# Moving the 32x32 inverses of a gated delta rule, and the transfers behind them, to GpSimd

## The chip, the cores and the metric

The kernel runs on one core of one Trainium2 chip. Times are device microseconds of a whole launch; each is the median of several runs. A core has five engines that work side by side, each with its own instruction order: TensorE (PE, matrix products; PEld is its weight load), VectorE (DVE), ScalarE (ACT), GpSimd (POOL) and SyncE (SP). An engine that issues a DMA does so in its own order, so an issue that waits holds up whatever stands behind it on that engine.

## The reference, cut to what matters

The reference is a two-block transformer on one sequence of 256 tokens, width 1024, all in f32: a gated DeltaNet layer, a convolutional MLP, sliding-window attention, a second MLP, and then a block with further mixers and an FFN. The change sits in the DeltaNet layer at the start. Its core solves one unit lower triangular system per chunk and head:

```python
    m = jnp.where(strict, jnp.einsum('bnhcd,bnhsd->bnhcs', k_beta, k) * decay, 0.0)
    eye = jnp.broadcast_to(jnp.eye(c, dtype=f32), m.shape)
    t_mat = lax.linalg.triangular_solve(m + eye, eye, left_side=True, lower=True,
                                        unit_diagonal=True)
    u = jnp.einsum('bnhcs,bnhse->bnhce', t_mat, v_beta)
    ...
    o = rmsnorm(o, out_norm_w) * jax.nn.silu(z)
    return o.reshape(bsz, t, GDN_V_DIM).astype(hn.dtype) @ w_out
```

The layer has 16 heads of 128. The kernel works with two chunks of 128 tokens.

## The kernel before

**Weights and products.** All weights arrive as 362 chunks of 128x1024 floats, in the order in which PE uses them, issued by SP (L172). ACT rounds each chunk to a high half wh (L186), DVE subtracts to get the low half wl (L187, two operands in SBUF), and every product of an activation with a weight is three matmuls (`mm3`, L249 to L251): xh·wh, xl·wh, xh·wl. The buffers let a few chunks run ahead of PE.

**Side work.** What is no weight product runs in generators. `tick` advances each of them by one `yield`; `w` calls it once per four weight tiles of 128 columns, which is twelve matmuls. So a stage that says `for _ in range(N): yield` lets N such pieces of weight work go ahead of it in the program. A tile scheduler then orders each engine's instructions from the program's order and the data that each needs. Nothing on the chip waits for a tick; the chip waits for data only.

**The inverse.** The q, k, v and z parts of `w_in` follow each other in the order of `ORDER`. From k, `x_stage` computes for each head three 128x128 blocks XA[:, h, 0..2] (chunk 0, the cross block, chunk 1). A 128x128 block is inverted from its four 32x32 diagonal blocks upward. `x_stage` stores the 4·2·16 diagonal blocks to DRAM s1, and `inv_stage` reads them back as NT with one block per partition (128 partitions, 32x32 each). Then 31 steps of substitution follow, each a product (fst, L757) and an addition into TI (L759), with one tick after each. TI is copied transposed to TP (L764). Both go to DRAM (s2, s3; `Q[2]`) and come back into place in 14 loads (`Q[3]`), eight into XA and six into T64, which lies in the tile h. `QS` says which engine issues each: `QS = "sgss"` means SP for s1, the two stores and the 14 loads, and GpSimd for NT.

**After the inverse.** `WINV` ticks later `st["inv"]` is set, and `chain(q4)` runs four times, for four heads each. It joins the blocks to 64 and then 128: y1p (L823) and z1p (L833, L834), with Y1 between them on ACT and DVE, then y2p and z2p. It then forms y0p, x10p, y1p (L879), the outputs o0p and o1p (L890 to L894), the gate and normalization on ACT and DVE, and the transposes otp (L921), whose results feed the product with `w_out`. `a_stage` runs beside it: one kq product (L729, L730) per pair of heads. The gate z goes through DRAM: GpSimd stores zt to wzd (L803) and loads it back as wzog (L886). A pool t2 of six buffers is shared by the convolution (cy), vt, zt, Y1, Y2 and r1.

Of the kernel before, what the change touches and what calls it, by code (L numbers as in the profile page):

```python
# [9 lines left out]
F32 = mybir.dt.float32  # L10
# [3 lines left out]
AF = mybir.ActivationFunctionType  # L14
ALU = mybir.AluOpType
# [4 lines left out]
P = 128  # L20
T = 256
# [98 lines left out]
CZ = 2  # L120
WSSB = 9
WVTP = 6
WINV = 10
ACCN = 4
SY1 = 5
SY2 = 5
# [8 lines left out]
XK = 0  # L135
NY = 4
NP = 2
QS = "sgss"
PINS = {1: 0, 3: 1}
ORDER = "qqzqqzvvvvvvzvvz"  # L140

# [1 line left out]
class Builder:  # L143
# [432 lines left out]
    def gdn_body(self, gp, x):  # L576
        nc, tc, sp = self.nc, self.tc, self.sp
# [3 lines left out]
        blk = lambda b: slice(32 * b, 32 * b + 32)  # L581
        ev2 = lambda b: b.rearrange("p (a t) -> p a t", a=2)
# [13 lines left out]
        ea = gp.tile([P, 1], F32, tag="ea", name="ea")  # L596
        fac = gp.tile([P, 5, 32], F32, tag="fac", name="fac")
        var, rk, irk, negc, rk2 = (fac[:, i] for i in range(5))
        XA = gp.tile([P, 16, 3, P], F32, tag="XA", name="XA")
        EA = gp.tile([P, 16, 3, P], F32, tag="EA", name="EA")  # L600
        vn = gp.tile([P, 2, 2048], F32, tag="vn", name="vn")
        st = {"bg": False, "kss": 0, "qss": 0, "X": 0, "v": 0, "inv": False, "z": 0, "A": 0, "lev": 0, "og": 0, "step": 0}
# [86 lines left out]

        Q = [{"s": nc.sync, "a": nc.scalar, "g": nc.gpsimd}[c] for c in QS]  # L690

        def x_stage():
            while st["kss"] < 4 or not st["bg"]:
                yield
            factors(0)
            for j in range(8):
                kk = self.bank("kk")
                nc.tensor.matmul(kk[:, 0:T], kT[:, j, 0:P], kT[:, j], start=True, stop=True)
                nc.tensor.matmul(kk[:, T:384], kT[:, j, P:], kT[:, j, P:], start=True, stop=True)
                for h in (2 * j, 2 * j + 1):  # L700
                    rp = self.bank("rp")
                    nc.tensor.matmul(rp[:, :384], identr[:, h : h + 1].to_broadcast([P, P]), gch, start=True, stop=False)
                    nc.tensor.matmul(rp[:, :384], identb, mask3b, start=False, stop=True)
                    nc.scalar.activation(EA[:, h, 0], rp[:, 0:128], AF.Exp, bias=bg[:, 0, 32 + h : 33 + h])
                    nc.scalar.activation(EA[:, h, 1], rp[:, 128:256], AF.Exp, bias=bg[:, 0, 64 + h : 65 + h])
                    nc.scalar.activation(EA[:, h, 2], rp[:, 256:384], AF.Exp, bias=bg[:, 1, 32 + h : 33 + h])
                    nc.vector.scalar_tensor_tensor(XA[:, h, 0:2], ev2(kk[:, 0:T]), negc[:, h : h + 1], EA[:, h, 0:2], ALU.mult, ALU.mult)
                    nc.vector.scalar_tensor_tensor(XA[:, h, 2], kk[:, T:384], negc[:, 16 + h : 17 + h], EA[:, h, 2], ALU.mult, ALU.mult)
                st["X"] = j + 1
                if j % 4 == 3:  # L710
                    H = slice(2 * j - 6, 2 * j + 2)
                    for b in range(4):
                        for tt in range(2):
                            Q[0].dma_start(s1[b, tt, H].rearrange("h s t -> s h t"), XA[blk(b), H, 2 * tt, blk(b)])
                if j % 4 != 3:
                    yield
                else:
                    for _ in range(4):
                        yield
# [19 lines left out]
        s1 = self.dp.tile([4, 2, 16, 32, 32], F32, name="s1")  # L739
        s2 = self.dp.tile([4, 2, 16, 32, 32], F32, name="s2")  # L740
        s3 = self.dp.tile([4, 2, 16, 32, 32], F32, name="s3")
        T64 = self.h.rearrange("p a t -> p (a t)").rearrange("p (a h c) -> p a h c", a=2, h=16)

        def inv_stage():
            while st["X"] < 8:
                yield
            NT = t4([P, 32, 32], "NT")
            TI = t4([P, 32, 32], "TI")
            Q[1].dma_start(NT, s1.rearrange("b c h s t -> (b c h) s t"))
            nc.gpsimd.memset(TI, 0.0)  # L750
            nc.gpsimd.memset(TI.rearrange("p a b -> p (a b)")[:, 0:1024:33], 1.0)
            for _ in range(INVW):
                yield
            for j in range(31):
                m = 31 - j
                tmp = gp.tile([P, 256], F32, tag="fst", bufs=1, name="fst")[:, : m * (j + 1)].rearrange("p (a b) -> p a b", a=m)
                nc.vector.tensor_tensor(tmp, NT[:, j, j + 1 :].unsqueeze(2).to_broadcast([P, m, j + 1]),  # L757
                                        TI[:, j, 0 : j + 1].unsqueeze(1).to_broadcast([P, m, j + 1]), ALU.mult)
                nc.vector.tensor_tensor(TI[:, j + 1 :, 0 : j + 1], TI[:, j + 1 :, 0 : j + 1], tmp, ALU.add)  # L759
                st["step"] = j + 1  # L760
                if INVS(j):
                    yield
            TP = t4([P, 32, 32], "TP")
            nc.vector.tensor_copy(TP.rearrange("p c i -> p i c"), TI)  # L764
            Q[2].dma_start(s3.rearrange("b c h s t -> (b c h) s t"), TP)
            Q[2].dma_start(s2.rearrange("b c h s t -> (b c h) s t"), TI)
            nc.gpsimd.memset(T64[0:32, :, :, 32:64], 0.0)
            for b in range(4):
                for tt in range(2):
                    Q[3].dma_start(XA[blk(b), :, 2 * tt, blk(b)], s3[b, tt].rearrange("h c i -> c h i"))  # L770
                    if b < 3:
                        c = (0, 32, 0)[b]
                        Q[3].dma_start(T64[blk(b), tt, :, c : c + 32], s2[b, tt].rearrange("h i c -> i h c"))
            for _ in range(WINV):
                yield
            st["inv"] = True
# [31 lines left out]
        hs = lambda i: slice(i * P, i * P + P)  # L808
        oks = {}

        def chain(q4):
            while not (st["inv"] and st["v"] >= 2 * q4 + 2 and st["lev"] >= q4):
                yield
            H = slice(4 * q4, 4 * q4 + 4)
            heads = range(4 * q4, 4 * q4 + 4)
            cs = slice(512 * q4, 512 * q4 + 512)
            Y1 = t2([P, 2, 4, 32], "Y1")
            b = self.bank("y1p")
            bv = b[:, 0:256].rearrange("p (a h c) -> p a h c", a=2, h=4)
            for tt in range(2):  # L820
                for i, h in enumerate(heads):
                    for j in (0, 2):
                        nc.tensor.matmul(bv[blk(j + 1), tt, i], XA[blk(j), h, 2 * tt, blk(j + 1)], T64[blk(j), tt, h, 0:32], start=True, stop=True)  # L823
            nc.scalar.activation(Y1[blk(1)], bv[blk(1)], AF.Copy)
            nc.vector.tensor_copy(Y1[blk(3)], bv[blk(3)])
            for _ in range(CY):
# [1 line left out]
            b = self.bank("z1p")  # L828
            bv = b.rearrange("p (k a h c) -> p k a h c", k=2, a=2, h=4)
            for tt in range(2):  # L830
                for i, h in enumerate(heads):
                    for j in (0, 2):
                        nc.tensor.matmul(bv[blk(j), 0, tt, i], Y1[blk(j + 1), tt, i], XA[blk(j + 1), h, 2 * tt, blk(j + 1)], start=True, stop=True)  # L833
                    nc.tensor.matmul(bv[blk(1), 1, tt, i], XA[blk(1), h, 2 * tt, blk(1)], Y1[blk(1), tt, i], start=True, stop=True)  # L834
            nc.scalar.activation(T64[blk(1), :, H, 0:32], bv[blk(1), 1], AF.Copy)
            for tt in range(2):
                nc.vector.tensor_copy(XA[blk(0), H, 2 * tt, blk(1)], bv[blk(0), 0, tt])
                nc.scalar.activation(XA[blk(2), H, 2 * tt, blk(3)], bv[blk(2), 0, tt], AF.Copy)
            for _ in range(CY):
                yield  # L840
            lo, hi = slice(0, 64), slice(64, 128)
            Y2 = t2([P, 2, 4, 64], "Y2")
            b = self.bank("y2p")
            bv = b.rearrange("p (a h c) -> p a h c", a=2, h=4)
            for tt in range(2):
                for i, h in enumerate(heads):
                    nc.tensor.matmul(bv[hi, tt, i], XA[lo, h, 2 * tt, hi], T64[lo, tt, h], start=True, stop=True)  # L847
            nc.scalar.activation(Y2[hi], bv[hi], AF.Copy)
            for _ in range(CY):
                yield  # L850
            b = self.bank("z2p")
            bv = b.rearrange("p (a h c) -> p a h c", a=2, h=4)
            for tt in range(2):
                for i, h in enumerate(heads):
                    nc.tensor.matmul(bv[lo, tt, i], Y2[hi, tt, i], XA[hi, h, 2 * tt, hi], start=True, stop=True)  # L855
            for tt in range(2):
                nc.vector.tensor_copy(XA[lo, H, 2 * tt, hi], bv[lo, tt])
            st["lev"] += 1
            for _ in range(CY):
                yield  # L860
# [2 lines left out]
            y = t4([P, 2, 512], "yy")  # L863
# [6 lines left out]
                yield  # L870
            b = self.bank("x10p")
            for i, h in enumerate(heads):
                nc.tensor.matmul(b[:, hs(i)], XA[:, h, 1], y[:, 0, hs(i)], start=True, stop=True)
            nc.vector.tensor_tensor(r1, b, vn[:, 1, cs], ALU.add)
            for _ in range(CZ):
                yield
            b = self.bank("y1p")
            for i, h in enumerate(heads):
                nc.tensor.matmul(b[:, hs(i)], XA[:, h, 2], r1[:, hs(i)], start=True, stop=True)  # L879
            nc.scalar.activation(y[:, 1], b, AF.Copy)  # L880
            while st["A"] < 2 * q4 + 2 or st["z"] < 2 * q4 + 2:
                yield
# [1053 lines left out]
```

## Time and profile before

| what | value |
|---|---|
| median of 3 runs | 1217.02 us (1215.78 to 1218.51) |
| the profiled execution's own time | 1216.23 us |
| its span, first to last instruction | 1214.4 us |
| granted TensorE clock, mean | 0.997 |
| PE busy | 1188.7 us, 98% of the span |
| DVE busy | 895.2 us, 74% |
| ACT busy | 687.7 us, 57% |
| POOL busy | 20.4 us, 2% |

The span lies 1.83 us inside the execution's own time. PE is nearly always busy; its idle time, and what ended each piece of it, is what a change beside it can alter. The averages cover 1214 us, while the inverse occupies some 60 to 80 us near the start, so the stretch from 100 to 210 us has to be read by itself. In the rows below a timeline gives start, duration, engine, line, operation, out<-in, and in brackets the idle time before it with what ended it.

### The profile page before, as it was taken

To read this page: it belongs to the slowest core of one execution; us is meant where nothing else is said; L and a number is where in the kernel's file an instruction comes from. 1 tells how busy PE (TensorE), PEld (TensorE's weight loads), DVE (VectorE), ACT (ScalarE), POOL (GpSimd) and SP (SyncE) were. 2 spreads that over 40 slices of the span, in tenths; PEclk is the share of its full clock that TensorE was granted. 3 is DMA by queue.
4 is the path that set the end of the run, shared out by engine and by line. 5 is a ranking of instruction groups with operands and counts; after the bars stand their busy time and mean duration, and the time that the engine had idled before them with its cause. 6 is when DMAs were issued, how large, how long until landed. Compare 5 with 4: busy or idle time off the path is not lost.

```text
span 1214.4 us, 23416 instructions
## 1 busy us (share of the span) xinstructions
PE 1188.7 (98%) x9368; PEld 1125.4 (93%) x9368; DVE 895.2 (74%) x1680; ACT 687.7 (57%) x1170; POOL 20.4 (2%) x47
## 2 busy tenths in 40 slices
PE   7999989999999999999999999999999999999997
PEld 6989878999999999889999999889789999999996
DVE  6978976668877778878977778756756567655555
ACT  5785547546655556656755556754465445444443
POOL 1000000000000000000000000000000000000000
PEclk9999999999999999999999999999999999999999
DMA  6546365355555557435555564364255563555552
GB/s 222 179 132 216 125 192 183 124 157 168 199 184 182 187 179 243 126 115 161 190 188 183 187 191 158 112 207 134 87 161 173 188 234 118 186 179 187 189 179 83
DMA packets 68318, 206.01 MB, mean 170 GB/s; under 512 B 18198, under 2 KB 18342, under 8 KB 67953
## 3 DMA queue, kind: packets, MB, share of 16 engines
q1 hardware_dynamic: 65600, 194.77, 50.3%
q0 software_dynamic: 2608, 9.75, 2.2%
q8 instruction: 73, 1.20, 0.4%
q14 instruction: 37, 0.29, 0.1%
HBM read 199.75 MB, written 4.74 MB: 168 GB/s over the span
## 4 chain that ended last, share of the span: by engine, by line
PE 92%; DVE 4%; ACT 2%; DMA 1%; issue 1%; SPq 0%; DVEq 0%; ACTq 0%
PE pb L249 21%; PE pb L250 20%; PE pb L251 20%; PE acc L249 7%; PE acc L250 7%; PE acc L251 7%; DVE wl L187 1%; PE pt L1138 1%; PE ssb L669 1%; DMA wr<-wall 0%; DMA h<-xT 0%; PE z2p L855 0%; PE y2p L847 0%; PE kv L1542 0%; PE csum L366 0%
## 5 line engine op out<-in xcount | busy, mean ns | idle before, releaser
L187 DVE TENSOR_TENSOR wl<-wr,wh 128x1024 fp32r<-128x1024 f32 x362 | 441.5, 1223 | 193.7 <-ACT wh L186 192.3
L186 ACT ACTIVATE wh<-wr 128x1024 fp32r<-128x1024 f32 x362 | 381.6, 1057 | 338.3 <-issue 101.1
L251 PE MATMUL pb<-xh,wl 128*128 128x256 f32 x1224 | 345.6, 283 | 3.9 <-DVE wl L187 3.9
L249 PE MATMUL pb<-xh,wh 128*128 128x256 f32 x1224 | 347.8, 284 | 0.6 <-ACT xh L569 0.6
L250 PE MATMUL pb<-xl,wh 128*128 128x256 f32 x1224 | 345.5, 282 | 0.2 <-DVE xl L570 0.2
L249 PEld LDWEIGHTS pb<-xh,wh 128*128 128x128 f32 x1224 | 231.7, 189 | 2.8 <-issue 1.3
L251 PEld LDWEIGHTS pb<-xh,wl 128*128 128x128 f32 x1224 | 229.7, 188 | 4.5 <-DVE wl L187 4.5
L250 PEld LDWEIGHTS pb<-xl,wh 128*128 128x128 f32 x1224 | 230.1, 188 | 0.5 <-DVE xl L570 0.4
L249 PE MATMUL pb<-fh,wh 128*128 128x256 f32 x416 | 118.3, 285 | 0.0
L250 PE MATMUL pb<-fl,wh 128*128 128x256 f32 x416 | 117.5, 283 | 0.1
L251 PE MATMUL pb<-fh,wl 128*128 128x256 f32 x416 | 116.6, 281 | 0.0
L249 PE MATMUL acc<-ah,wh 128*128 128x256 f32 x352 | 98.7, 280 | 0.0
L251 PE MATMUL acc<-ah,wl 128*128 128x256 f32 x352 | 98.5, 280 | 0.0
L250 PE MATMUL acc<-al,wh 128*128 128x256 f32 x352 | 98.5, 280 | 0.0
L249 PEld LDWEIGHTS pb<-fh,wh 128*128 128x128 f32 x416 | 77.9, 188 | 1.4 <-issue 0.4
L250 PEld LDWEIGHTS pb<-fl,wh 128*128 128x128 f32 x416 | 78.1, 188 | 1.1 <-DVE fl L436 0.3
L251 PEld LDWEIGHTS pb<-fh,wl 128*128 128x128 f32 x416 | 78.9, 190 | 0.0
L977 DVE SCALAR_TENSOR_TENSOR fy<-fpad,cols,fy 128x256 f32<-128x256 f32 x176 | 73.6, 478 | 0.0
L249 PE MATMUL pb<-wh,xh 128*128 128x512 f32 (+1 forms) x176 | 70.5, 402 | 0.0
L250 PE MATMUL pb<-wl,xh 128*128 128x512 f32 (+1 forms) x176 | 68.1, 387 | 0.5 <-DVE wl L187 0.5
L251 PE MATMUL pb<-wh,xl 128*128 128x512 f32 (+1 forms) x176 | 68.0, 387 | 0.0
L249 PEld LDWEIGHTS acc<-ah,wh 128*128 128x128 f32 x352 | 66.9, 190 | 0.0
(437 smaller groups left out, 2091.2 us busy)
## 6 DMA issues: line engine op xcount, KB each, us to landing
wr<-wall SPq DMA_DIRECT2D x362, 512.0 KB, 3.6
wzd<-zt POOLq DMA_DIRECT2D x8, 256.0 KB, 3.0
wzog<-wzd POOLq DMA_DIRECT2D x4, 512.0 KB, 5.2
bias<-bd POOLq DMA_DIRECT2D x4, 512.0 KB, 7.7
h<-xT SPq DMA_DIRECT2D x4, 256.0 KB, 4.0
h<-xT POOLq DMA_DIRECT2D x1, 1024.0 KB, 5.9
wrow<-wrow POOLq DMA_DIRECT2D x1, 1024.0 KB, 10.0
out_dram<-mw SPq DMA_DIRECT2D x4, 256.0 KB, 2.0
```

What stands on the lines that cost most here:

```text
L186: nc.scalar.activation(hi, r, AF.Copy)
L187: i = nc.vector.tensor_tensor(lo, r, hi.bitcast(F32), ALU.subtract)
L249: mm(out, ah, bh, start=start, stop=False, skip_group_check=skip)
L250: mm(out, ah, bl, start=False, stop=False, skip_group_check=skip)
L251: mm(out, al, bh, start=False, stop=stop, skip_group_check=skip)
L669: nc.tensor.matmul(ssb[:, c : c + 1], sq[:, i, tt * P : tt * P + P], self.ones[:, 0:1], start=True, stop=True)
L977: nc.vector.scalar_tensor_tensor(y[:, i], u[:, i, j : j + T], w(j), y[:, i], ALU.mult, ALU.add)
L1138: nc.tensor.transpose(pt[:, j * P : j * P + P], S[:, i, j * P : j * P + P], self.ident)
```

## The change

The 62 operations of the substitution and the transposing copy run on GpSimd instead of DVE. `QS` becomes "sggg": the stores to s2 and s3 and the loads behind them are issued by GpSimd instead of SP. XA is stored with the block index ahead of the head and with the two chunks' blocks next to each other, so one load fills both chunks: 7 loads of 128 KB in place of 14 of 64 KB. All index expressions follow (`2 * tt` becomes `tt`, the cross block is 2 instead of 1). `WINV` goes from 10 to 16.

```diff
-WINV = 10
+WINV = 16
-QS = "sgss"
+QS = "sggg"
...
-        XA = gp.tile([P, 16, 3, P], F32, tag="XA", name="XA")
+
+        XAb = gp.tile([P, 3, 16, P], F32, tag="XA", name="XA")
+        XA = XAb.rearrange("p k h c -> p h k c")
...
-                nc.vector.tensor_tensor(tmp, NT[:, j, j + 1 :].unsqueeze(2).to_broadcast([P, m, j + 1]),
+                nc.gpsimd.tensor_tensor(tmp, NT[:, j, j + 1 :].unsqueeze(2).to_broadcast([P, m, j + 1]),
                                         TI[:, j, 0 : j + 1].unsqueeze(1).to_broadcast([P, m, j + 1]), ALU.mult)
-                nc.vector.tensor_tensor(TI[:, j + 1 :, 0 : j + 1], TI[:, j + 1 :, 0 : j + 1], tmp, ALU.add)
+                nc.gpsimd.tensor_tensor(TI[:, j + 1 :, 0 : j + 1], TI[:, j + 1 :, 0 : j + 1], tmp, ALU.add)
...
-            nc.vector.tensor_copy(TP.rearrange("p c i -> p i c"), TI)
+            nc.gpsimd.tensor_copy(TP.rearrange("p c i -> p i c"), TI)
             Q[2].dma_start(s3.rearrange("b c h s t -> (b c h) s t"), TP)
             Q[2].dma_start(s2.rearrange("b c h s t -> (b c h) s t"), TI)
...
-                for tt in range(2):
-                    Q[3].dma_start(XA[blk(b), :, 2 * tt, blk(b)], s3[b, tt].rearrange("h c i -> c h i"))
-                    if b < 3:
-                        c = (0, 32, 0)[b]
-                        Q[3].dma_start(T64[blk(b), tt, :, c : c + 32], s2[b, tt].rearrange("h i c -> i h c"))
+                Q[3].dma_start(XAb[blk(b), 0:2, :, blk(b)].rearrange("p k h c -> p (k h) c"), s3[b].rearrange("a h c i -> c (a h) i"))
+                if b < 3:
+                    c = (0, 32, 0)[b]
+                    Q[3].dma_start(T64[blk(b), :, :, c : c + 32].rearrange("p a h c -> p (a h) c"), s2[b].rearrange("a h i c -> i (a h) c"))
...
-                        nc.tensor.matmul(bv[blk(j + 1), tt, i], XA[blk(j), h, 2 * tt, blk(j + 1)], T64[blk(j), tt, h, 0:32], start=True, stop=True)
+                        nc.tensor.matmul(bv[blk(j + 1), tt, i], XA[blk(j), h, tt, blk(j + 1)], T64[blk(j), tt, h, 0:32], start=True, stop=True)
```

Lines of the changed kernel are one or two higher than before (y1p L824, z1p L834). On SP, before, the two stores and the 14 loads stand among the weight loads (s_208 and s_209 are the DRAM tiles s2 and s3):

```order
L172 DMA wr_1867<-wall 128x1024
L766 DMA s_208<-TI 128x1024
L765 DMA s_209<-TP 128x1024
L172 DMA wr_1892<-wall 128x1024
L773 DMA h<-s_208 32x16x32
L770 DMA XA<-s_209 32x16x32 x2
L773 DMA h<-s_208 32x16x32
L770 DMA XA<-s_209 32x16x32
```

After, only weight loads are left on SP. On GpSimd, after, the substitution begins behind the clearing of TI, around a pair of stores of z:

```order
L752 MEMSET TI 128x1024
L753 MEMSET TI 128x32
L759 ISA
L759 TENSOR_TENSOR fst<-NT,TI 128x31
L804 DMA wzd<-zt 128x512
L761 TENSOR_TENSOR TI<-TI,fst 128x31
L804 DMA wzd<-zt 128x512
L759 TENSOR_TENSOR fst<-NT,TI 128x60
```

The first addition stands behind one of these stores and the second product behind the other. On the same engine, after, this is the end of the substitution:

```order
L761 TENSOR_TENSOR TI<-TI,fst 128x31
L766 COPY TP<-TI 128x32x32
L768 DMA s_208<-TI 128x1024
L767 DMA s_209<-TP 128x1024
L774 DMA h<-s_208 32x32x32
L771 DMA XA<-s_209 32x32x32 x2
L774 DMA h<-s_208 32x32x32
L771 DMA XA<-s_209 32x32x32
L774 DMA h<-s_208 32x32x32
L771 DMA XA<-s_209 32x32x32
L804 DMA wzd<-zt 128x512 x2
L887 DMA wzog<-wzd 128x1024 x2
```

The copy, two stores and seven loads now stand in one queue, and the next stores of z and the loads of the gate stand behind them. On PE, before, 15 of the 16 matmuls of the first join (y1p, of h and XA) follow the sixth of the eight kq at a distance of three weight products (pb), and the first z1p comes at once behind them:

```order
L729 MATMUL kq<-qT,kT 128x256
L730 MATMUL kq<-qT,kT 128x128
L249 MATMUL pb<-xh,wh_1919 128x256
L250 MATMUL pb<-xl,wh_1919 128x256
L251 MATMUL pb<-xh,wl_1920 128x256
L823 MATMUL y1p<-h,XA 32x32 x15
L833 MATMUL z1p<-XA,Y_1976 32x32
```

On PE, after, the same join follows the seventh kq:

```order
L731 MATMUL kq<-qT,kT 128x256
L732 MATMUL kq<-qT,kT 128x128
L824 MATMUL y1p<-h,XA 32x32 x16
L249 MATMUL pb<-xh,wh_1974 128x256
L250 MATMUL pb<-xl,wh_1974 128x256
L251 MATMUL pb<-xh,wl_1975 128x256
L249 MATMUL pb<-wh_2023,xh 128x512
```

The first join moved from the sixth kq to the seventh, at once behind it, and weight products come between it and z1p. Further on, on PE, before, weight products stand between the first output o0p and its companion o1p (o0p and o1p are the two outputs of a group of heads; two more groups of six follow before otp):

```order
L890 MATMUL o0p<-yy,EA 128x128 x4
L855 MATMUL z2p<-XA,Y_2288 64x64 x8
L823 MATMUL y1p<-h,XA 32x32 x16
L249 MATMUL pb<-wh_2202,xh 128x512
L250 MATMUL pb<-wl_2203,xh 128x512
L251 MATMUL pb<-wh_2202,xl 128x512
```

On PE, after, at the same place:

```order
L848 MATMUL y2p<-h,XA 64x64 x8
L880 MATMUL y1p<-r_2281,XA 128x128 x4
L891 MATMUL o0p<-yy,EA 128x128 x4
L856 MATMUL z2p<-XA,Y_2338 64x64 x8
L824 MATMUL y1p<-h,XA 32x32 x16
L894 MATMUL o1p<-yy,EA 128x128
L895 MATMUL o1p<-yy,EA 128x128
```

From o0p to otp there is no weight product any more; the three groups of six stand ahead of it.

## Rows read from the trace of the kernel before

**Rows 1.** Page: part 1 (busy, share, instructions) and chain shares by engine

```profile
PE 1188.7 (98%) x9368; PEld 1125.4 (93%) x9368; DVE 895.2 (74%) x1680; ACT 687.7 (57%) x1170; POOL 20.4 (2%) x47
...
PE 92%; DVE 4%; ACT 2%; DMA 1%; issue 1%; SPq 0%; DVEq 0%; ACTq 0%
```

**Rows 2.** Timeline of PE, 139 to 179 (start, us, what; idle before, releaser)

```profile
139.51 0.39 PE L251 MATMUL pb<-xh,wl 128*128 128x256 f32 x1 [1.47 <-DVE wl L187]
...
154.03 0.51 PE L250 MATMUL pb<-wl,xh 128*128 128x512 f32 x1 [0.49 <-DVE wl L187]
...
160.60 0.33 PE L789 MATMUL vtp<-ident,vt 128*128 128x128 f32 x1 [1.14 <-ACT vt L651]
...
169.75 0.21 PE L833 MATMUL z1p<-XA,Y 32*32 32x32 f32 x1 [0.46 <-ACT Y L824]
...
178.07 0.39 PE L251 MATMUL pb<-xh,wl 128*128 128x256 f32 x1 [1.72 <-DVE wl L187]
```

**Rows 3.** Windows: per stretch length, busy of PE, PEld, DVE, ACT, POOL

```profile
100.00:130.00 30.00, 30.00 (x235) 29.03 (x234) 28.07 (x68) 16.75 (x25) 1.08 (x2) 1.00 0.60 190
130.00:160.00 30.00, 27.50 (x175) 24.08 (x173) 29.72 (x79) 15.14 (x25) 0.00 (x0) 1.00 0.50 153
```

**Rows 4.** Lines of DVE, 100 to 160 (busy, mean ns; idle)

```profile
L187 DVE TENSOR_TENSOR wl<-wr,wh 128x1024 fp32r<-128x1024 f32 x18 | 21.7, 1216 | 1.3 <-ACT wh L186 1.3
...
L759 DVE TENSOR_TENSOR TI<-TI,fst 128x31 f32<-128x31 f32 (+15 forms) x31 | 10.4, 336 | 0.2
...
L757 DVE TENSOR_TENSOR fst<-NT,TI 128x31 f32<-128x31 f32 (+15 forms) x31 | 10.3, 333 | 0.1
...
L764 DVE COPY TP<-TI 128x1024 f32<-128x1024 f32 x1 | 1.1, 1146 | 0.0
```

**Rows 5.** Timeline of SP's DMA queue, 150 to 163

```profile
150.67 0.33 SPq L766 DMA_DIRECT2D s<-TI  x1
...
162.99 86.68 SPq L172 DMA_DIRECT2D wr<-wall  x19
```

**Rows 6.** Timeline of POOL, the instructions nearest to the change

```profile
7.13 0.30 POOL L589 CAST identb<-ident 128x128 bf16<-128x128 f32 x1 [5.54 <-DMA ident<-cst]
...
21.08 0.66 POOL L588 CAST mask3b<-mask 128x384 bf16<-128x384 f32 x1
...
97.17 0.15 POOL L751 MEMSET TI<- 128x32 f32 x1
...
106.27 0.54 POOL L803 DMA_DIRECT2D wzd<-zt  x1 [0.16 <-issue]
```

**Rows 7.** DVE beside the cast; line L187, ns min/median/max

```profile
21.31 1.52 DVE L187 TENSOR_TENSOR wl<-wr,wh 128x1024 fp32r<-128x1024 f32 x1
...
L187 DVE TENSOR_TENSOR wl<-wr,wh x362: 1202/1225/1520, 10.7 to 1198.2; 128x1024 fp32r<-128x1024 f32 x181
```

**Rows 8.** Line L1045: issue of a transfer of 512 runs

```profile
L1045 POOL DMA_DIRECT2D bias<-bd x4: 748/754/800, 469.9 to 472.2; - x4
```

**Rows 9.** DMA view: issues, KB each, median us to landing

```profile
s<-TI SPq DMA_DIRECT2D x1, 512.0 KB, 3.6
...
XA<-s SPq DMA_DIRECT2D x8, 64.0 KB, 3.9
...
h<-s SPq DMA_DIRECT2D x6, 64.0 KB, 2.9
```

**Rows 10.** Timeline of PE: seventh kq, then o0p and otp

```profile
175.29 0.38 PE L729 MATMUL kq<-qT,kT 128*128 128x256 f32 x1
...
195.56 1.06 PE L890 MATMUL o0p<-yy,EA 128*128 128x128 f32 x8
...
198.24 0.50 PE L249 MATMUL pb<-wh,xh 128*128 128x512 f32 x1
...
199.74 0.38 PE L893 MATMUL o1p<-yy,EA 128*128 128x128 f32 x2
...
208.52 0.66 PE L921 MATMUL otp<-ident,wzog 128*128 128x128 f32 x4
```

More of the change, by code (lines that the diff above doesn't have):

```diff
@@ L706, in x_stage @@
                     nc.scalar.activation(EA[:, h, 2], rp[:, 256:384], AF.Exp, bias=bg[:, 1, 32 + h : 33 + h])
-                    nc.vector.scalar_tensor_tensor(XA[:, h, 0:2], ev2(kk[:, 0:T]), negc[:, h : h + 1], EA[:, h, 0:2], ALU.mult, ALU.mult)
-                    nc.vector.scalar_tensor_tensor(XA[:, h, 2], kk[:, T:384], negc[:, 16 + h : 17 + h], EA[:, h, 2], ALU.mult, ALU.mult)
+                    nc.vector.scalar_tensor_tensor(XA[:, h, 0:3:2], ev2(kk[:, 0:T]), negc[:, h : h + 1], EA[:, h, 0:2], ALU.mult, ALU.mult)
+                    nc.vector.scalar_tensor_tensor(XA[:, h, 1], kk[:, T:384], negc[:, 16 + h : 17 + h], EA[:, h, 2], ALU.mult, ALU.mult)
                 st["X"] = j + 1
@@ L713, in x_stage @@
                         for tt in range(2):
-                            Q[0].dma_start(s1[b, tt, H].rearrange("h s t -> s h t"), XA[blk(b), H, 2 * tt, blk(b)])
+                            Q[0].dma_start(s1[b, tt, H].rearrange("h s t -> s h t"), XA[blk(b), H, tt, blk(b)])
                 if j % 4 != 3:
@@ L832, in chain @@
                     for j in (0, 2):
-                        nc.tensor.matmul(bv[blk(j), 0, tt, i], Y1[blk(j + 1), tt, i], XA[blk(j + 1), h, 2 * tt, blk(j + 1)], start=True, stop=True)
-                    nc.tensor.matmul(bv[blk(1), 1, tt, i], XA[blk(1), h, 2 * tt, blk(1)], Y1[blk(1), tt, i], start=True, stop=True)
+                        nc.tensor.matmul(bv[blk(j), 0, tt, i], Y1[blk(j + 1), tt, i], XA[blk(j + 1), h, tt, blk(j + 1)], start=True, stop=True)
+                    nc.tensor.matmul(bv[blk(1), 1, tt, i], XA[blk(1), h, tt, blk(1)], Y1[blk(1), tt, i], start=True, stop=True)
             nc.scalar.activation(T64[blk(1), :, H, 0:32], bv[blk(1), 1], AF.Copy)
             for tt in range(2):
-                nc.vector.tensor_copy(XA[blk(0), H, 2 * tt, blk(1)], bv[blk(0), 0, tt])
-                nc.scalar.activation(XA[blk(2), H, 2 * tt, blk(3)], bv[blk(2), 0, tt], AF.Copy)
+                nc.vector.tensor_copy(XA[blk(0), H, tt, blk(1)], bv[blk(0), 0, tt])
+                nc.scalar.activation(XA[blk(2), H, tt, blk(3)], bv[blk(2), 0, tt], AF.Copy)
             for _ in range(CY):
@@ L846, in chain @@
                 for i, h in enumerate(heads):
-                    nc.tensor.matmul(bv[hi, tt, i], XA[lo, h, 2 * tt, hi], T64[lo, tt, h], start=True, stop=True)
+                    nc.tensor.matmul(bv[hi, tt, i], XA[lo, h, tt, hi], T64[lo, tt, h], start=True, stop=True)
             nc.scalar.activation(Y2[hi], bv[hi], AF.Copy)
@@ L854, in chain @@
                 for i, h in enumerate(heads):
-                    nc.tensor.matmul(bv[lo, tt, i], Y2[hi, tt, i], XA[hi, h, 2 * tt, hi], start=True, stop=True)
+                    nc.tensor.matmul(bv[lo, tt, i], Y2[hi, tt, i], XA[hi, h, tt, hi], start=True, stop=True)
             for tt in range(2):
-                nc.vector.tensor_copy(XA[lo, H, 2 * tt, hi], bv[lo, tt])
+                nc.vector.tensor_copy(XA[lo, H, tt, hi], bv[lo, tt])
             st["lev"] += 1
@@ L872, in chain @@
             for i, h in enumerate(heads):
-                nc.tensor.matmul(b[:, hs(i)], XA[:, h, 1], y[:, 0, hs(i)], start=True, stop=True)
+                nc.tensor.matmul(b[:, hs(i)], XA[:, h, 2], y[:, 0, hs(i)], start=True, stop=True)
             nc.vector.tensor_tensor(r1, b, vn[:, 1, cs], ALU.add)
@@ L878, in chain @@
             for i, h in enumerate(heads):
-                nc.tensor.matmul(b[:, hs(i)], XA[:, h, 2], r1[:, hs(i)], start=True, stop=True)
+                nc.tensor.matmul(b[:, hs(i)], XA[:, h, 1], r1[:, hs(i)], start=True, stop=True)
             nc.scalar.activation(y[:, 1], b, AF.Copy)
```

## The prediction, made before the changed kernel was timed

> **What bounds the kernel now.** The first view is the page's busy shares with the chain that ended last [rows 1]: PE is busy for 98% of the span and holds 92% of that chain, so only idle time of PE can be won, or added. The chain also holds DVE at 4%: PE now and then waits for wl, the low half of a weight chunk, which DVE splits off. Next I read PE's timeline over the stretch in which the substitution runs and its result is first used, 139 to 179 us. It has five idles [rows 2]: 1.47, 0.49 and 1.72 us for wl, 1.14 us for vt and 0.46 us for Y, together 5.28 us. Why wl is late there is seen in the windows: from 100 to 160 DVE is busy 28.07 + 29.72 = 57.8 of 60 us [rows 3]. By its lines, 18 wl take 21.7 us of that, the 62 operations of the substitution 10.4 + 10.3 = 20.7 us, and the transposing copy 1.1 us [rows 4]. SP's queue is the third view: between the first store (150.67) and the next free run of weight loads (162.99) it issues two stores and fourteen small loads, with one weight load among them [rows 5].
>
> **What is taken away.** DVE loses 20.7 + 1.1 = 21.8 us and keeps 57.8 − 21.8 = 36.0 of 60 us. With that much room a wl is no longer queued behind a substitution step, so I take the three wl idles as gone (3.68 us). vt and Y come from ACT, and stand in the stretch where SP's loads and a full DVE hold up weights and bank readers; I take them as gone too. Together −5.28 us. The bounds of this term: nothing at all, if the reordered program brings the same idles back at other places, and about −8, half as much again, if gaps of PE too small for the timeline shrink too (an estimate). SP's 12.3 us of queue go as well, at no value of their own, since no idle in [rows 2] names a late weight load; the work that hides them is the weight loads already in flight.
>
> **What GpSimd pays.** Step j multiplies and adds (31−j)(j+1) elements per partition, 5456 over the 31 steps, so 10,912 elements in 62 operations. The trace of before has no such operation on this engine. The nearest rows are its casts: 0.66 us for 384 elements and 0.30 us for 128 [rows 6], a slope of 0.36/256 = 1.41 ns per element and 0.12 us that does not depend on size. With one input that is 10,912 × 1.41 + 62 × 0.12 = 15.4 + 7.4 = 22.8 us. If the second input costs as much as the first, 30.8 + 7.4 = 38.2 us. DVE's own 20.7 us is the low end. I take 34 us, nearer to the upper row, because every operation here reads two operands. [...]
>
> The first add stands behind one of a pair of wzd stores in GpSimd's order and the second multiply behind the other, which before starts at 106.27 and takes 0.54 us [rows 6]: start 106.8, end 141 if nothing disturbs it. The order also has a new instruction in front of the first multiply that carries no operands (ISA). Its cost is unknown; TI is cleared by 97.17 + 0.15 = 97.3 and the second of the pair of stores goes at 106.27 [rows 6], so up to 8 us of it are hidden, and what goes beyond adds one for one to the times below.
>
> It will be disturbed. One cast of GpSimd ran beside DVE's split: cast 21.08 to 21.74, wl from 21.31, and this wl took 1.52 us, the longest of 362 whose median is 1.225 [rows 6, 7]. So wl lost 0.30 us to a GpSimd read. [...] In the other direction, 18 wl × 0.3 = 5.4 us come back on DVE, which then has 41 of 60 us: still no cause for idles.
>
> **The tail behind it.** In one queue, in order: the transposing copy (DVE 1.15 us [rows 4]; here about 1.5), two stores, one of which must land (median 3.6 us [rows 9]; about 4), then the loads. A GpSimd transfer of 128 runs is issued in 0.54 us [rows 6], one of 512 runs in 0.754 [rows 8]; along that line one of 1024 runs takes 1.04. The first joining product needs six of the seven loads: five issues ahead × 1.04 = 5.2, then a landing, 2.9 to 3.9 us for half the size [rows 9], about 4, at most 8. Together 1.5 + 4 + 5.2 + 4 = 14.7 us. [...]
>
> **When PE asks.** In the changed order the first y1p stands behind the seventh kq, not the sixth, with the same PE work ahead of it as the seventh kq had. That kq starts at 175.29 [rows 10]; the four idles before it [rows 2] are 3.56 us, and the kq itself takes about 0.65 us (0.38 for its wider product, the same row): 172.4. [...]
>
> **What is squeezed.** The shift of y1p pushes the chain of joins closer to its use. Between the first o0p and the first otp before, 13.0 us pass [rows 10], with three groups of six products of a weight chunk and one of four transposes between. Six such products take 199.74 − 198.24 = 1.50 us [rows 10]; in the new order all three groups, 4.5 us, and the transposes are elsewhere, and only about 8 us of PE work are left. otp waits for squares, a gate and a normalization on ACT and DVE that hang on o1p. How much of the 13.0 us they need the trace does not say, since PE never waits there: between 0 and 4.8 us. I take +2. The third pair of wzd stores now stands behind the seven loads in GpSimd's queue, and two loads of wzog behind it, so zt buffers come free later, by the length of the tail at most. I price that at nothing, because the next use of these buffers is the joins themselves; if not, it is part of the same +2.
>
> **Sum.** −5.3 + 2.0 + 0 (loads just in time) = −3.3 us. The profiled execution took 1216.23 us, so 1212.9; it lies 0.79 below the median of the runs, 1217.02, so about 1213.7 as a median.
>
> **The rivals.**
> - Slower: GpSimd delivers late and PE stands at the first y1p. It decides from a substitution that ends after 161: then y1p waits over 3.3 us and the gain is gone. [...] The GpSimd cast beside wl [rows 7] and the bound of 38.2 speak for it, the low ends against it.
> - No change: only the idles ahead of y1p go (−3.6), and the squeeze takes 2 to 4.8, or the data are 2 to 3 us late: 1215.5 to 1218.5. For it: PE is at 98%, and removed idles tend to come back at the next tight place.
> - More gain: the squeeze costs nothing and the small gaps go too, −5.3 to −8: 1209.5 to 1211.7. For it: DVE at 99% from 130 to 160. Against it: the shortened o-stage.
> [...]
>
> **How the numbers follow.** Forecast (data in time, squeeze about 2, including the last rival) 0.48, by itself 1211.5 to 1215.5; more gain 0.08; no change 0.17; slower 0.27. What a measurement of this kernel can tell from no change is 0.2%, 2.4 us; the forecast's −3.3 is only just beyond it, so 0.08 of its 0.48 counts as the same, and 0.03 of the no-change case falls on each side. Faster 0.40 + 0.08 + 0.03 = 0.51, same 0.08 + 0.11 = 0.19, slower 0.27 + 0.03 = 0.30. The range takes in the larger gain and most of the slower case: 1209.5 to 1223.
>
> **What would show it.** The idles of [rows 2] should be gone and DVE should have about 40 of 60 us. GpSimd's adds and multiplies should grow with elements at 1.4 to 2.8 ns each where no wl runs, and wl should be longer than 1.225 us beside them. [...] The wait ahead of the first y1p, and the releaser named there (a load of h or XA), decides the sign; the wait ahead of otp shows the squeeze. The forecast is wrong if PE stands for more than 3 us at y1p, or if idles of the kind in [rows 2] are still there although DVE has room.

## The result: slower by 0.7%

The changed kernel takes 1226.59 us (5 runs) against 1216.65 of before (5 runs), a ratio of 1.0071 with a 95% interval of 1.0049 to 1.0094. The forecast was 1213.7 and the range ended at 1223. The profiled execution took 1226.85 us, its span is 1225.1.

The page's first lines of the changed kernel answer to [rows 1]:

```profile
PE 1195.5 (98%) x9368; PEld 1132.1 (92%) x9368; DVE 885.2 (72%) x1617; ACT 688.3 (56%) x1170; POOL 75.7 (6%) x119
...
PE 93%; DVE 3%; ACT 2%; DMA 1%; issue 1%; POOL 0%; SPq 0%; DVEq 0%; ACTq 0%
```

PE is still 98% busy: for the same 9368 matmuls it is busy 6.8 us longer than before and idle 3.9 us longer. Its timeline shows the longest idle at the seventh kq, and another further on at otp:

```profile
171.06 0.59 PE L731 MATMUL kq<-qT,kT 128*128 128x256 f32 x2
...
173.03 0.22 PE L824 MATMUL y1p<-h,XA 32*32 32x32 f32 x2 [1.15 <-DMA h<-s]
180.46 1.06 PE L824 MATMUL y1p<-h,XA 32*32 32x32 f32 x30 [7.22 <-DMA h<-s]
...
216.01 0.30 PE L922 MATMUL otp<-ident,wzog 128*128 128x128 f32 x1 [1.33 <-DVE wzog L914]
```

The idles of [rows 2] are gone, and the seventh kq comes 4.2 us earlier than in [rows 10]. Then PE stands 8.4 us for loads of h. The windows of the same kernel (columns as in [rows 3]; behind the busy times the granted clock as a share of full speed, the DMA engines' share, GB/s) show a second price and, in the first two, DVE:

```profile
100.00:130.00 30.00, 30.00 (x230) 28.86 (x229) 24.55 (x43) 18.26 (x26) 21.11 (x30) 1.00 0.65 221
130.00:160.00 30.00, 30.00 (x202) 27.47 (x201) 27.07 (x50) 17.95 (x31) 27.27 (x36) 1.00 0.48 159
...
170.00:175.00 5.00, 2.10 (x17) 1.77 (x15) 3.60 (x8) 0.05 (x1) 5.00 (x8) 1.00 0.96 211
175.00:180.00 5.00, 0.00 (x0) 0.00 (x0) 0.00 (x0) 0.00 (x0) 0.36 (x1) 0.65 1.04 185
180.00:185.00 5.00, 4.54 (x40) 3.90 (x41) 1.55 (x2) 2.43 (x4) 0.00 (x0) 0.50 0.17 66
185.00:190.00 5.00, 5.00 (x66) 3.54 (x65) 2.41 (x5) 2.27 (x4) 0.00 (x0) 0.83 0.32 108
...
215.00:220.00 5.00, 3.77 (x21) 3.64 (x22) 3.50 (x14) 2.28 (x5) 0.54 (x1) 0.74 0.01 3
```

After the wait PE works at 0.50 of full speed, and at 0.83 in the next five us; before, the clock was 1.00 in every window from 170 to 220, as in these two:

```profile
180.00:185.00 5.00, 5.00 (x71) 4.44 (x69) 3.61 (x7) 1.91 (x3) 0.00 (x0) 1.00 0.89 293
185.00:190.00 5.00, 5.00 (x73) 4.24 (x72) 3.79 (x8) 3.68 (x8) 0.00 (x0) 1.00 0.54 192
```

At 0.50 the 128x512 weight products start 0.43 us apart (182.26, 182.69, 183.11), before and at 1.00 0.23 to 0.24 (192.57, 192.80, 193.03, 193.27). Half of 4.5 us of work and a sixth of 5 are some 3 us, an estimate from the clock of the two windows. Another dip, to 0.74, follows the wait at otp.

The start-up of this profiled execution is 1.6 us later than that of before, by the first kk product (59.0 and 60.6 us), ahead of anything changed. Below, the **net shift** of a run is how much later its attention stage starts (the first score product after the layer, at 488.3 before), less how much later the first kk starts; it leaves such differences out, but it describes one execution. For the changed kernel it is 9.4 − 1.6 = +7.8 us.

GpSimd's timeline in the changed kernel gives the three pieces of the lateness:

```profile
141.47 0.70 POOL L761 TENSOR_TENSOR TI<-TI,fst 128x240 f32<-128x240 f32 x1
142.25 1.45 POOL L759 TENSOR_TENSOR fst<-NT,TI 128x231 f32<-128x231 f32 x1
...
159.24 0.25 POOL L761 TENSOR_TENSOR TI<-TI,fst 128x31 f32<-128x31 f32 x1
159.56 2.13 POOL L766 COPY TP<-TI 128x1024 f32<-128x1024 f32 x1
...
162.08 0.53 POOL L767 DMA_DIRECT2D s<-TP  x1
164.74 0.82 POOL L774 DMA_DIRECT2D h<-s  x1 [2.13 <-DMA s<-TI]
169.56 1.58 POOL L771 DMA_DIRECT2D XA<-s  x2 [4.00 <-DVE cy L652]
...
172.69 0.79 POOL L774 DMA_DIRECT2D h<-s  x1
```

The substitution ends at 159.5. Operations of like size take 0.70 or 1.45 us: of the 62, 16 are over 1.2 us long. DVE beside these two has a wl in which each loses time to the other (the median wl takes 1.225 us [rows 7], and the other product of the second one's size, which began at 123.24 just ahead of a wl, 0.59):

```profile
141.54 1.71 DVE L187 TENSOR_TENSOR wl<-wr,wh 128x1024 fp32r<-128x1024 f32 x1 [0.38 <-ACT wh L186]
```

The loads of XA start only at 169.6. The profile names a DVE operation there, but the store of TP has landed just before (162.08 + 6.9), and in every run below whose GpSimd issues both, the XA loads start 0.6 us after that landing. The DMA view has that store, and the loads, of twice the size, at 1.8 and 2.8 times the landing time of [rows 9]:

```profile
s<-TP POOLq DMA_DIRECT2D x1, 512.0 KB, 6.9
XA<-s POOLq DMA_DIRECT2D x4, 128.0 KB, 6.9
h<-s POOLq DMA_DIRECT2D x3, 128.0 KB, 8.1
```

Which load ends the wait is worth a look. The first y1p starts at 173.03, when the first h load has landed and no XA load has (the quickest takes 6.0 us, 169.56 + 6.0 = 175.5). So the first join reads nothing that the XA loads bring; its blocks of XA lie off the diagonal (z1p, behind it, reads those that are loaded). The load that ends the wait is the third h, which needs only the store of TI, landed at 164.5. It is issued at 172.69 because it stands sixth in the queue, behind three XA loads that wait for the copy and for the store of TP. No run here puts the three h loads first.

### The profile page after: what moved, and what is told of

It reads as the page before. It is cut to its first block, busy times and chain, and to the rows that moved or that the text cites. A ratio compares the mean times of both kernels' runs of the same rounds, so it can differ in the third digit from the quotient of the medians.

```text
span 1225.1 us, 23420 instructions
## 1 busy us (share of the span) xinstructions
PE 1195.5 (98%) x9368; PEld 1132.1 (92%) x9368; DVE 885.2 (72%) x1617; ACT 688.3 (56%) x1170; POOL 75.7 (6%) x119
## 4 chain that ended last, share of the span: by engine, by line
PE 93%; DVE 3%; ACT 2%; DMA 1%; issue 1%; POOL 0%; SPq 0%; DVEq 0%; ACTq 0%
PE pb L249 21%; PE pb L250 21%; PE pb L251 20%; PE acc L249 7%; PE acc L250 7%; PE acc L251 7%; DMA h<-s 1%; DVE wl L187 1%; PE pt L1139 1%; PE ssb L671 1%; PE csum L366 0%; ACT wh L186 0%; DMA ident<-cst 0%; PE o0p L891 0%; PE z2p L856 0%
## 5 line engine op out<-in xcount | busy, mean ns | idle before, releaser
L187 DVE TENSOR_TENSOR wl<-wr,wh 128x1024 fp32r<-128x1024 f32 x362 | 444.6, 1232 | 212.9 <-ACT wh L186 211.6
```

The lines of the kernel that those rows point to most:

```text
L187: i = nc.vector.tensor_tensor(lo, r, hi.bitcast(F32), ALU.subtract)
```

## The experiments

Diffs are against the changed kernel unless said. Ratios are to the kernel before, run beside each.

**1. The arithmetic back on DVE, all else as changed.**

```diff
-                nc.gpsimd.tensor_tensor(tmp, NT[:, j, j + 1 :]...
+                nc.vector.tensor_tensor(tmp, NT[:, j, j + 1 :]...
```

(the addition and the copy likewise)

> The changed kernel with the substitution and the transposing copy back on DVE; queues, seven loads and WINV 16 stay. Theory A (GpSimd's arithmetic ends 10 us too late): the substitution ends near 150 as before, the loads land near 171, the 8.4 us wait at y1p and the clock dip behind it go, the wl idles of before (3.7 us) come back; near 1217 to 1219 (the squeezed o-stage costs about 2). Rival B (the transfers on GpSimd's queue are what is late, whoever computes): y1p still waits 5 us or more, 1223 or above.

1221.48 us, ratio 1.0023 (1.0009 to 1.0037), net shift +0.3. PE's waits (in total, times, longest):

```profile
PE otp L922 <- DVE wzog L914: 1.5, 2, 1.3
PE z1p L834 <- ACT Y L825: 1.5, 1, 1.5
PE pb L251 <- DVE wl L187: 1.5, 1, 1.5
```

The y1p wait and the dip are gone, and wl is late again (1.5 us here and 0.5 at another product), as theory A has it. The same loads from the same queue, begun 9.7 us earlier, land at 168.6, before PE asks at 174.2: without GpSimd's slower arithmetic they are not late. The time, though, lies between the two theories. The profiled execution took 1218.05 us, one of the three shortest of ten, and its trace shows 0.3 of the 2.8 us that the ratio gives; the rest stays open.

**2. The transfers back on SP, the arithmetic on GpSimd.**

```diff
-QS = "sggg"
+QS = "sgss"
```

> The changed kernel with the stores and the seven loads issued by SP again. Theory A: the substitution ends at 159 to 160 as in the changed kernel and the small runs drain in about 11 us whoever issues them, so y1p waits 6 to 10 us and the time stays at 1222 to 1228. Rival B (GpSimd's slow issue and its queue make the loads late): the wait falls by 5 us or more, 1217 to 1220.

1236.84 us, ratio 1.0150 (1.0133 to 1.0167), net shift +20.0. Neither theory had this. SP's queue, and PE:

```profile
126.14 0.33 SPq L172 DMA_DIRECT2D wr<-wall  x1
154.88 0.33 SPq L767 DMA_DIRECT2D s<-TP  x1
```

```profile
164.75 1.11 PE L790 MATMUL vtp<-ident,vt 128*128 128x128 f32 x4 [17.74 <-ACT vt L653]
```

The store of TP stands at SP's head for 28.4 us until GpSimd is through, with the weight loads behind it, and PE runs dry. Moving the arithmetic alone would have been worse; the queues had to go with it. The seven loads, as large as in the changed kernel, land here in 3.5 to 4.5 us each where they take 6.0 to 8.2 there. So they do not drain alike whoever issues them; but fewer weight loads were in flight here too, and no run separates the two.

**3. Fourteen steps on GpSimd, then seventeen on DVE.**

```diff
+                eng = nc.gpsimd if j < 14 else nc.vector
```

> The first 14 substitution steps on GpSimd, the other 17 and the copy on DVE; transfers as in the changed kernel. Theory A: GpSimd is through at about 131, DVE at about 148 to 152, the loads land near 170 and PE asks at about 172: no wait above 2 us at y1p, no clock dip there, 1212 to 1216. Rival B (transfers): a wait of 5 us or more is left, 1220 or above.

1228.08 us, ratio 1.0076 (1.0061 to 1.0092), net shift +9.4; no wait at y1p, but an earlier one. DVE, then PE:

```profile
127.11 0.43 DVE L760 TENSOR_TENSOR fst<-NT,TI 128x255 f32<-128x255 f32 x1 [7.98 <-POOL TI L762]
```

```profile
128.70 1.11 PE L791 MATMUL vtp<-ident,vt 128*128 128x128 f32 x4 [6.37 <-ACT vt L653]
```

DVE's first own step was ordered ahead of other work, stood 8 us for GpSimd, and the convolution and the wl behind it waited too. The expectation had overlooked the order.

**4. The first join eight ticks later.**

```diff
-WINV = 16
+WINV = 24
```

> The changed kernel with WINV 24: the first join stands 11.5 us of weight products later, the o-stage where it was. Theory A (only the lateness counts, 8.4 us, and the clock that falls in the wait): the wait at y1p goes, 1213 to 1217. Rival C (the joins need that time themselves): the idle moves into the joins y1p to otp, each waiting for ACT or DVE, with as much idle in sum, 1220 or above.

1228.17 us, ratio 1.0074 (1.0059 to 1.0089), net shift +11.6: rival C by its time and its idles (9.2 us in the joins and at otp). The y1p wait is gone, z1p waits instead, and ACT's timeline gives a cause that the rival had not named:

```profile
PE z1p L834 <- ACT Y L825: 5.0, 1, 5.0
```

```profile
186.96 1.06 ACT L888 ACTIVATE wzog<-wzog 128x1024 f32<-128x1024 f32 x1 [6.28 <-DMA wzog<-wzd]
```

ACT stands for the gate's load, which GpSimd issued behind the seven loads, at 177.5; Y is behind it on ACT, at 190.07. Then the clock is 0.50 for 20 us:

```profile
190.00:200.00 10.00, 7.09 (x115) 6.27 (x116) 4.52 (x8) 5.41 (x11) 1.09 (x2) 0.51 0.49 159
200.00:210.00 10.00, 10.00 (x95) 9.16 (x94) 1.16 (x3) 2.58 (x6) 0.00 (x0) 0.50 0.01 2
```

**5. No wl beside the substitution.**

```diff
+        skip = 28 <= j <= 44
+        lo = self.halves[j - 1][1] if skip else self.wtile(j, F32R, "wl")
```

> The changed kernel without the split on DVE for weight chunks 28 to 44, the ones that fall beside the substitution: their products use the low half of chunk 27, so the low halves of 17 chunks are left out. Theory L (each GpSimd operation that begins beside a wl waits for it): the 16 operations of 1.3 to 1.6 us shrink to the 0.25 to 0.75 of the others, the 62 operations take 31 to 33 us in place of 46.9 and the substitution ends at 142 to 146 in place of 159.5; the wait at y1p is gone. Rival (the long operations are GpSimd's own): 16 long ones stay, end near 158.

1215.99 us in one run. GpSimd's lines (busy, mean ns), the end of the substitution, and y1p:

```profile
L763 POOL TENSOR_TENSOR TI<-TI,fst 128x31 f32<-128x31 f32 (+15 forms) x31 | 17.0, 547 | 2.4
L761 POOL TENSOR_TENSOR fst<-NT,TI 128x31 f32<-128x31 f32 (+15 forms) x31 | 16.2, 524 | 5.8 <-DMA NT<-s 3.5
```

```profile
143.48 0.25 POOL L763 TENSOR_TENSOR TI<-TI,fst 128x31 f32<-128x31 f32 x1
```

```profile
170.65 0.69 PE L826 MATMUL y1p<-h,XA 32*32 32x32 f32 x32
```

33.2 us in place of 46.9, no operation over 1.2 us, no wait at y1p: theory L. Yet the net shift is only −1.0, and 1215.99 lies within the range of the kernel before, run beside it (1215.90 to 1220.75). The data are early here and most of the gain still goes, in the shortened o-stage: waits of 2.2 and 0.8 us at otp and a clock of 0.83 from 200 to 210.

**6. Useless products in the wait.**

```diff
+                for _ in range(9):
+                    nc.tensor.matmul(fb, self.ident, kT[:, 0:2].rearrange("p a t -> p (a t)"), start=True, stop=True)
```

> The changed kernel with nine idle products (f32, 128x128 by 512, about 0.87 us each, 7.8 us in sum) put before the first y1p, where PE would otherwise stand: useless work in a wait that is there anyway. Theory K (the wait costs twice, once by itself and once by the clock of 0.5 to 0.83 granted from 175 to 190): the granted clock stays at 1.00 through 170 to 200 and the time falls by about 3 us, to 1223. Rival (the clock after the wait costs nothing, as PE waits for the joins anyway): the time stays within 1 us of the changed kernel's 1226.6 or rises.

1222.89 us, ratio 1.0039 (1.0028 to 1.0049), 0.32% less than the changed kernel, some 3.9 us; net shift +5.6, 2.3 less. PE and two windows:

```profile
170.12 7.89 PE L821 MATMUL fill<-kT,ident 128*128 128x512 f32 x18
...
179.15 0.69 PE L828 MATMUL y1p<-h,XA 32*32 32x32 f32 x30 [0.97 <-DMA h<-s]
```

```profile
180.00:185.00 5.00, 5.00 (x71) 3.96 (x71) 3.33 (x7) 3.38 (x6) 0.00 (x0) 1.00 0.28 69
185.00:190.00 5.00, 5.00 (x35) 4.18 (x34) 3.70 (x8) 2.49 (x6) 1.07 (x2) 1.00 0.62 212
```

Busy for nothing, PE keeps its clock, 1.00 in both windows: theory K. y1p goes ahead no sooner after the seventh kq than in the changed kernel, so what is gained is gained behind it: from the 30 y1p to otp 32.6 us pass in place of 35.6. The clock is 2 to 4 us of the loss. The clock itself is shown by the windows; the times alone would not settle it, since the intervals of the two ratios meet at 1.0049.

**7. Half the runs in each load.**

```diff
-XAb[blk(b), 0:2, :, blk(b)]... s3[b]...
+XAb[blk(b), 0:1, :, blk(b)]... s3[b, 0:1]...
```

> The changed kernel with the seven loads cut to the first chunk's half, 512 runs of 128 bytes each in place of 1024; the second chunk's inverse blocks are left out. Theory R (the loads drain at a rate per run, about 11 us for the seven): the last load that y1p needs lands at 175 to 177 in place of 180.4 and the wait falls by 4 to 5 us. Rival F (each load on this queue takes 7 to 8 us to land, whatever its size): it lands at 179.5 or later, the wait falls by 1 us or less.

1221.44 us in one run. GpSimd and PE:

```profile
162.44 1.34 POOL L774 DMA_DIRECT2D h<-s  x2 [2.13 <-DMA s<-TI]
...
167.97 1.93 POOL L771 DMA_DIRECT2D XA<-s  x3 [4.20 <-DVE cy L652]
```

```profile
175.27 1.06 PE L824 MATMUL y1p<-h,XA 32*32 32x32 f32 x30 [5.04 <-DMA h<-s]
```

From the first XA load to y1p 7.3 us pass, against 180.46 − 169.56 = 10.9, and the wait falls by 3.2 us, to 5.2: theory R in direction, less than expected, and not rival F. A price per run cannot be read off, because the edit also moved a load. Two h loads now go ahead of the XA loads, so four loads of 512 runs are issued up to the one that is needed, where the changed kernel issues five of 1024. And the two ahead still take 7.1 and 7.4 us to land with half the runs, where the first h load of the changed kernel takes 8.2.

**8. Only WINV 16, in the kernel before.**

```diff
-WINV = 10
+WINV = 16
```

> The kernel before with WINV 16 in place of 10 and nothing else: the squeeze by itself. Theory S (from the first o0p to otp only 4 to 5 us of PE work are left; PE waits there and its clock dips): waits of about 1.5 to 2.2 us at otp and a dip of the granted clock at 205 to 215, the wl idles of before stay; 2 to 4 us slower than before. Rival (later joins cost nothing on DVE's timetable): within 1 us of before, no wait at otp.

1223.48 us, ratio 1.0049 (1.0033 to 1.0065), net shift +4.5. Waits of PE and one window:

```profile
PE pb L249 <- ACT wh L186: 3.2, 1, 3.2
PE pb L251 <- DVE wl L187: 1.9, 2, 1.4
PE otp L921 <- DVE wzog L913: 1.5, 2, 1.3
...
170.00:180.00 10.00, 6.35 (x60) 5.77 (x60) 7.92 (x13) 5.37 (x7) 0.00 (x0) 0.71 0.31 91
```

The otp wait is there as theory S has it, without a dip behind it; the larger part is a wait for wh and the dip with it, at 170 to 180, which no theory had. So WINV 16 has a price of its own on DVE's timetable, 6.0 us by the ratio and more than theory S had, but only a third of the net shift is shown to be the squeeze.

**9. Seventeen steps on DVE, then fourteen on GpSimd.**

```diff
+                eng = nc.vector if j < 17 else nc.gpsimd
```

> The first 17 substitution steps on DVE, the last 14 and the copy on GpSimd, so that no DVE instruction waits for GpSimd. Theory A: DVE is through with its part at 122 to 128, GpSimd with its at 146 to 152, the loads land at 167 to 173, PE asks at 172 to 175: no wait above 2 us at y1p, no clock dip there; wl idles smaller than before; 1214 to 1218. Rival B (the transfers or the shorter o-stage set the time): 1219 or above.

1215.65 us, ratio 0.9978 (0.9968 to 0.9987), net shift −2.3: faster than both. GpSimd ends at 150.2; PE's waits and two windows:

```profile
PE otp L923 <- DVE wzog L915: 1.5, 2, 1.3
PE vtp L791 <- ACT vt L653: 0.4, 1, 0.4
PE x10p L875 <- ACT yy L870: 0.2, 1, 0.2
...
170.00:175.00 5.00, 5.00 (x54) 3.87 (x53) 4.21 (x10) 2.43 (x4) 0.00 (x0) 1.00 0.74 297
...
200.00:210.00 10.00, 8.29 (x90) 7.71 (x92) 6.90 (x28) 4.39 (x16) 0.54 (x1) 0.83 0.09 20
```

With half the steps on each, the data are in time, no wl is late, and no DVE instruction waits for GpSimd. What is left is the wait at otp with its dip.

**10 to 12. Closer joins on top of 9**, to give otp more work ahead of it (and loads in the block order 0, 2, 1, 3).

```diff
-CY = 2
-CZ = 2
+CY = 1
+CZ = 1
```

> The kernel with 17 steps on DVE and 14 on GpSimd, its loads in the order of blocks 0, 2, 1, 3, and one tick in place of two between the joins and between y0p, x10p and y1p. Theory S: with the first o0p about 4.7 us earlier in PE's work and otp 3 us later, the wait at otp and the clock dip at 200 to 210 go, about 3 us gained on the 1215.65 of that kernel, 1212 to 1213.5. Rival J (joins one tick apart wait for ACT and DVE in between): new waits at z1p, y2p or x10p of 3 us or more in sum, 1216 or above.

1215.93 us, ratio 0.9985 (0.9976 to 0.9995). The otp wait falls to 0.5 us, and z1p waits 2.0 for Y with a clock of 0.83 from 170 to 180. Theory S is missed, and so, narrowly, are rival J's bounds; the new wait is of its kind.

> As the one with one tick between all steps, but with two ticks kept between y0p, x10p and y1p. Theory S: o0p where it was, otp 4 us of PE work later, so the wait at otp goes as well, 1212 to 1214. Rival J: z1p stands 0.9 us of work behind y1p and waits 1 us or more there, y2p and z2p likewise, 1215.5 or above.

1218.17 us, ratio 1.0002 (0.9991 to 1.0013): z1p waits 2.5, x10p 1.1; rival J again.

> The kernel with 17 steps on DVE and 14 on GpSimd and one tick between the joins, but two again between y1p and z1p. Theory S: z1p stands 3.0 us of work behind y1p and no longer waits (2.0 us and the dip at 170 to 180 in the one-tick kernel go), otp stands 7.3 us of work behind o0p in place of 4.5 and waits less than 0.7 us without a dip: 1211 to 1214. Rival J: the idles come back at y2p, z2p or further on as waits of 2 us or more in sum, 1215 or above.

1215.23 us, ratio 0.9976 (0.9966 to 0.9987), not to be told from experiment 9: z1p no longer waits, but x10p does, 1.7 us in sum. The idle moved on, as rival J has it, though the time stayed.

## Why the prediction was wrong, point by point

- **What bounds the kernel, and what is taken away**: right in sign. PE's idles went, DVE has 51.6 of 60 us against 57.8, more than the 41 forecast, since other work moved up into the room. Up to the seventh kq the gain is 4.2 + 1.6 of start-up = 5.8 us where 3.6 was forecast: the named idles were not all of it, the small gaps count. (In the rival with more gain, −8 from 1217.0 is 1209.0 and not 1209.5; nothing hangs on it.)
- **What GpSimd pays**: right for the operations by themselves. With no wl beside them the 62 take 33.2 us (experiment 5; forecast 34). In the changed kernel the undisturbed additions grow from 0.25 us for 31 elements to 0.75 for 256, 2.2 ns per element, the products from 0.24 to 0.62, 1.7 ns, inside the 1.4 to 2.8 of the forecast. Beside wl the whole lasts from 107.7 to 159.5, 51.8 us; the end, 159.5, is 157.9 when the later start-up is taken off, against the forecast's 141 if nothing disturbs it. What disturbs it is shown: 16 wl fell into the stretch and 16 operations were long (1.3 to 1.6 us), each of them began while a wl ran, ended 0.1 to 0.5 us after it, and in experiment 5 none was left; where GpSimd began first, wl grew to 1.71 us. The rows of before show DVE's side alone, 0.30 us in one wl [rows 7].
- **The tail behind it** is the step that failed: 14.7 us forecast, 180.4 − 159.5 = 20.9 measured. Its two landings were sized wrong, at 4 us each: the store of TP landed after 6.9 and the last load needed after 7.7, together 6.6 more. The copy took 2.1 where 1.5 was forecast, and 1.0 us passed between the pieces. Against that, the issues ahead of the last load took 3.1 us where 5.2 was forecast (0.79 each, not 1.04, and one load went ahead). I had taken the landings of [rows 9] as they were and as independent of each other. Why they grew is shown only in part. With fewer and smaller loads the batch is quicker (experiment 7). The same loads land in half the time in experiment 2, issued by SP with fewer weight loads in flight. And the store of TP takes 3.9 us in experiments 1 and 3, where DVE makes the copy and the two stores are issued 1.1 us apart, against 6.4 to 7.6 in the changed kernel and in all other runs in which GpSimd issues them, 0.6 us apart. One cause that fits the loads and is not tested is SP's freed queue, to which the forecast gave no value: before, SP issued no weight load between 154.04 and 162.99, since the inverse's transfers stood in its queue; after, it issued them at 162.6, 164.6, 168.1 and 171.0, beside these transfers, and from 170 to 180 the DMA engines are full (shares of 0.96 and 1.04).
- **When PE asks**: 171.9 for 172.4, but that it came so near is luck. With the later start-up taken off it is 170.3, 2.1 us sooner than forecast, because the small gaps went too. So the sum's "loads just in time" became 8.4 us of wait, some 6 from the tail and 2 from PE. No run shows the 0 of that term: with the forecast's tail it asks for a substitution that ends by 172.4 − 14.7 = 157.7, and the changed kernel showed an end at 159.5, a tail of 20.9 and the wait in its place. That is the slower rival's place and releaser, but not its condition: it asked for a substitution that ends after 161, and this one ended at 159.5. The forecast put the clock at nothing as well: the wait of 7.2 us cost 2 to 4 us more after it ended (experiment 6), and the time, 1226.59, lies beyond the range's 1223.
- **What is squeezed**: forecast +2. The waits are 1.5 us at otp, as forecast, but the dip to 0.74 behind them was not. In experiment 5, with early data, the seventh kq leads by 5.8 us (169.9 against 175.3, and 0.4 of start-up), and a net 1.0 is left. With the idle of 1.7 us of before that is saved behind it, 6.5 us are lost there; otp's waits (3.0), the dip (1.7) and x10p (0.2) are 4.9 of them. The other 1.6 stay open, since PE's order differs too much there to follow them.
- The two accounts meet: from the seventh kq to the attention stage the changed kernel loses 9.4 + 4.2 = 13.6 us. The wait is 8.4, the clock some 4.5 (an estimate from the windows), otp 1.5, x10p 0.2, and the one idle of [rows 2] that lay behind the seventh kq (1.72) is saved: 12.9. About 0.7 us is not assigned.

## What to carry to other kernels

A transfer's landing should not be taken from another moment: the same loads landed in 3.5 to 4.5 us in experiment 2 and in 6.0 to 8.2 in the changed kernel. Who issued them and how many weight loads were in flight both differed, and no run separates the two, so the price should ask for both, and for what the change itself sets free to run there. On SP in experiment 2 an issue that waited held up those behind it for 28.4 us, so the loads that the first reader needs should not stand behind loads that wait for something else (here not tested). Work taken from a full engine should be split so that the slower engine gets only what it can finish in time, and comes last, so that nothing waits for it in the faster engine's order: 1215.65 us with GpSimd last (experiment 9), 1228.08 with GpSimd first, where DVE stood 8 us for it (experiment 3). And a wait on PE in which the clock falls, as in the 7.2 us here, has to be priced twice.

## What the runs showed of the hardware that was not expected

In the wait of 7.2 us, which began at 173.2, the granted clock fell: 1.00 from 175 to 176, 0.74 in the next us, 0.50 from 177 to 186, and 1.00 again from 187, some 10 us after it had fallen and 6.5 us after PE had begun to work again. In experiment 4 it stayed at 0.50 from 190 to 210, with short waits of PE up to 199.4 and none from there to 210. Waits of 1.5 to 2 us sometimes brought a dip (0.74 in the changed kernel, 0.83 in experiments 9 and 10) and sometimes none (1.00 behind otp in experiment 8). A wl on DVE and an operation of the substitution on GpSimd that overlapped cost time on both sides: GpSimd operations of 0.3 to 0.7 us became 1.3 to 1.6, and wl of 1.2 us became up to 1.7.
